# A hybrid decoder layer on one core: in 27 panels an accumulating DMA makes the low part of one weight tile in four

## Chip, core and metric

One NeuronCore of a Trainium2 chip runs the whole layer (batch 1, 256 tokens, width 1024). The metric is device time of one execution in microseconds (us): 602.37 us before the change, the median of three runs (602.12 to 602.67).

## What is computed

The reference is one layer, in float32:

```python
h  = rms_norm(x, ln1_g)
q, k, v, z, xbc, dt_raw, gate_a, gate_b = split(h @ w_in)
y_a = moba_attention(rms(q), rms(k), v) @ w_o_attn
y_b = mamba2_mixer(z, xbc, dt_raw, ...) @ w_o_ssm
x  = x + (sigmoid(gate_a) * y_a + sigmoid(gate_b) * y_b) @ w_out
h2 = rms_norm(x, ln2_g)
g, u = split(h2 @ w_gate_up)
x  = x + (silu(g) * u) @ w_down
x  = x + (p @ w_ple_proj) * sigmoid(rms_norm(x, ln3_g) @ w_ple_gate)
```

Nearly all of the arithmetic is products of 256 tokens with weight matrices of 1024 or more rows, about 100 MB of weights in all.

## The kernel before

**Products in two parts.** TensorE takes its operands as float32r, a rounded float32. To keep precision, the kernel splits each weight W into a high part Wh (W rounded) and a low part Wl = W - Wh, and each activation likewise into Ah and Al. A product A W is then three matmuls into the same PSUM bank: Ah Wh, Ah Wl and Al Wh. The names in the code and in the profile are `wh`, `wl`, `raw` (the weight as it was loaded) and `s` (all the activations, tiles of the tag `s4`).

**Panels.** The weights are cut into panels of 512 output columns and 1024 rows. A panel has eight k blocks of 128 rows. It is computed for two token tiles of 128, so it takes 8 x 2 x 3 = 48 matmuls of 128x512 into two PSUM tiles `g`. The class `Panel` (L333) does this: `add` (L345) walks over four k blocks, `step` (L365) issues the three matmuls of one block for one token tile. The loop at L903 runs over the panels of the input projection (`PANELS`, L34: xbc, q, k, v, z and the gates; an entry `yb` is a shorter panel of the mixer's output projection, done in `ssm_out`, L863). The loop at L1041 runs over the panels 2 to 10 of gate and up of the feed-forward part, here called the FFN panels. The panels of attention output, `w_out`, `w_down` and the last projection are written out elsewhere.

**Loads and splits.** A chunk of four k blocks comes as two DMAs of 512 KB (two k blocks each) into `raw`, from SyncE's queue (L275, in `load`, L269). For each tile ScalarE writes `wh` by a rounding copy (`act`, L151) and VectorE writes `wl` by a subtraction (`split_w`, L260, the subtraction at L263). There are 4 buffers for `raw`, 3 for `wh` and 6 for `wl` (L256 to L258).

**Order of the work.** Between the matmuls of the panels stand the smaller steps of the layer: transposes (L192, by a product with `ident`), the products of attention and of the scan, each waiting for ScalarE and VectorE. A `Filler` (L78) interleaves them: after each step of a panel `fill.step()` runs one piece of a waiting task, if its delay has passed on a counter of matmul time (`fill.now`). The table `LAG` (L68) holds these delays in ns. Panel matmuls keep their order among themselves (`main=True`). A scheduler then fixes the order of each engine's queue by priorities and its own clock.

**GpSimd** does little: a power of -0.5 for the norms (L381, L571) and masks for the scan (L635).

Of the kernel before, what the change touches and what calls it, by code (L numbers as in the profile page):

```python
# [10 lines left out]
F32 = mybir.dt.float32  # L11
F32R = mybir.dt.float32r
AF = mybir.ActivationFunctionType
ALU = mybir.AluOpType
AX = mybir.AxisListType

P = 128
T = 256
# [47 lines left out]


LAG = {  # L68
    "dt": 9198, "dt.t": 3823, "dt.e": 24762, "dt.low": 2074, "dt.end": 6965, "xbc": 3815, "xbc.t": 1507,
    "xbc.end": 7967, "z": 7477, "z.t": 2878, "z.end": 2196, "qk": 21856, "qk.t": 1263, "qk.end": 1856,  # L70
    "v": 3215, "cb": 0, "rows": 538, "prep": 3126, "seg": 492, "seg.next": 11553, "out": 13590,
    "out.xdt": 4839, "out.end": 90, "off": 3340, "off.end": 560, "finish": 6082, "finish.ones": 3453,
    "sc": 6834, "sc.tr": 2218, "tr": 0, "tr.val": 759, "val": 2876, "val.end": 3654, "m": 1401, "res": 4378,
    "ff": 1875, "ff.end": 1668,
}


# [31 lines left out]
def tile_layer(ctx: ExitStack, tc: tile.TileContext, head, xk, pt, vec, w_dt, w_big, w_dn2, w_pp, out):  # L109
    nc = tc.nc  # L110
# [3 lines left out]
    @contextmanager  # L114
    def prio(c):
        saved = tc.cur_priority
        tc.cur_priority = counters[c]
        yield
        counters[c] = tc.cur_priority
        tc.cur_priority = saved  # L120

    const = ctx.enter_context(tc.tile_pool(name="const", bufs=1))
    sb = ctx.enter_context(tc.tile_pool(name="sb", bufs=1))
    psg = ctx.enter_context(tc.tile_pool(name="psg", bufs=4, space=bass.MemoryType.PSUM))
    psb = ctx.enter_context(tc.tile_pool(name="psb", bufs=4, space=bass.MemoryType.PSUM))
    fill = Filler()
    uid = [0]

    def nm(s):
        uid[0] += 1  # L130
        return f"{s}_{uid[0]}"

    def s4(shape, dt=F32):
        return sb.tile([P] + shape, dt, tag="s4", bufs=26, name=nm("s4"))
# [15 lines left out]
    def act(o, i, f=AF.Copy, **kw):  # L150
        return nc.scalar.activation(o, i, f, **kw)  # L151
# [4 lines left out]
    def queue(ins, main):  # L156


        if fill.last is not None:
            follow(ins, fill.last)  # L160
        if main:
            fill.last = ins
# [6 lines left out]
    def mm(o, lhsT, rhs, start, stop, main=False):  # L169
        ins = nc.tensor.matmul(o, lhsT, rhs, start=start, stop=stop).ins  # L170
        queue(ins, main)
        passes = 4 if lhsT.dtype == F32 else 1
        fill.now += passes * max(107.0, rhs.free_size() / 2.4)
        return ins
# [58 lines left out]
    v = const.tile([P, V_N], F32, name="vecs")  # L233
# [19 lines left out]
    chunk_no = [0]  # L253

    def w_tiles():
        return (sb.tile([P, 2, 512], F32, tag="raw", bufs=4, name=nm("raw")),  # L256
                sb.tile([P, 2, 512], F32R, tag="wh", bufs=3, name=nm("wh")),
                sb.tile([P, 2, 512], F32R, tag="wl", bufs=6, name=nm("wl")))  # L258

    def split_w(tiles, js=slice(0, 2), c=WHOLE):  # L260
        raw, wh, wl = (t[:, js, c] for t in tiles)
        rounded = act(wh, raw)
        nc.vector.tensor_sub(wl, raw, wh.bitcast(F32))  # L263
        return rounded

    def parts_of(tiles):
        return [(tiles[1][:, j], tiles[2][:, j]) for j in range(2)]

    def load(src, nk):  # L269

        with prio("w"):
            parts = []
            for k in range(0, nk, 2):
                tiles = w_tiles()
                nc.sync.dma_start(tiles[0], src[:, k : k + 2])  # L275
                split_w(tiles)
                parts += parts_of(tiles)
        return parts
# [38 lines left out]
    def next_chunk():  # L317
        c = w_big[chunk_no[0]]
        chunk_no[0] += 1
        return load(c, 4)  # L320


    hh = [s4([4, T], F32R) for _ in range(2)]
    hl = [s4([4, T], F32R) for _ in range(2)]
    h_act = [(hh[k // 4][:, k % 4], hl[k // 4][:, k % 4]) for k in range(8)]

    def split_h(k):
        g = g1[:, k : k + 1]
        xk_ = xraw[k // 2][:, k % 2] if k else x0[:, 8:]
        tc.keep_in_program_order(act(h_act[k][0], xk_, scale=g))  # L330
        stt(h_act[k][1], xk_, g, h_act[k][0].bitcast(F32), op0=ALU.mult, op1=ALU.subtract)

    class Panel:  # L333

# [10 lines left out]
        def add(self, parts, acts, last):  # L345
            n = len(parts)
            if last:
                runs = [(pc, k) for pc in self.pieces for k in range(n)]
            else:
                runs = [(pc, k + j) for k in range(0, n, 2) for pc in self.pieces for j in range(2)]  # L350
            for pc, k in runs:
                self.step(pc, parts[k], acts[k], last and k == n - 1)

        def open(self, part, act_, cs):

            for w, w_acts in zip(part, (act_[:2], act_[:1])):
                for c in cs:
                    for a in w_acts:
                        for tt, _, ps in self.pieces:
                            with prio("mm"):  # L360
                                mm(ps[:, c], a[:, tt * P : tt * P + P], w[:, c], w is part[0] and a is act_[0] and c is cs[0] and id(self.pieces[tt]) not in self.begun, False, main=True)
            self.begun.update(id(pc) for pc in self.pieces)
            fill.step()
# [499 lines left out]
    def ssm_out(g):  # L863

        fill.drain(lambda: g in y_hl)
        yh, yl = y_hl[g]
        for n in range(2):
            if g == 0:
                accs[n] = s4([2, 512])
            acc = accs[n]  # L870
            pan = Panel()
            pan.add(next_chunk(), [(yh[:, k], yl[:, k]) for k in range(4)], last=True)
            with prio("ev"):
                for tt in range(2):
                    r = r_ssm[:, g, tt : tt + 1]
                    if g == 0:
                        act(acc[:, tt], pan.ps[tt], scale=r)
                    else:
                        stt(acc[:, tt], pan.ps[tt], r, acc[:, tt], op0=ALU.mult, op1=ALU.add)

    def evacuate(kind, i, pan):
        gen = evac[kind](kind, i, pan)
        t = next(gen)
        fill.spawn(gen, 0, t - fill.now)
# [3 lines left out]
    for k in range(0, 8, 2):  # L888
# [3 lines left out]
        for ks, bs in ([((k,), (0, 1)), ((k + 1,), (0, 1))] if k < 4 else [((k, k + 1), (0,)), ((k, k + 1), (1,))]):  # L892
            for b in bs:
# [6 lines left out]
                if k == 6:  # L900
                    evacuate(*PANELS[b][:2], pans[b])

    for kind, i, _ in PANELS[2:]:  # L903
        if kind == "yb":
            ssm_out(i)
            continue
        pan = Panel()
        for hf in range(2):
            pan.add(next_chunk(), h_act[4 * hf : 4 * hf + 4], last=hf == 1)
        evacuate(kind, i, pan)  # L910


# [35 lines left out]
    for n in range(2):  # L948
        pan = Panel()
# [56 lines left out]
    for n in range(2):  # L1006
        pan = Panel()
# [6 lines left out]
    ff = []  # L1014
# [23 lines left out]

    pair(res2.acts, evac_gu)
    h2 = res2.acts[0] + res2.acts[1]  # L1040
    for i in range(2, NFF):  # L1041
        pan = Panel()
        for hf in range(2):
            pan.add(next_chunk(), h2[4 * hf : 4 * hf + 4], last=hf == 1)
        evac_gu(i, pan)

    res3 = Residual(xin, V_G3, rstd3)
    for n in range(2):
        pan = Panel()
# [92 lines left out]
```

## Time and profile before

| | |
|---|---|
| Median of 3 runs (lowest, highest) | 602.37 us (602.12, 602.67) |
| Span of the profiled execution | 600.7 us, about 1.7 us under the median, for what lies around the span |
| TensorE busy, weight loads busy | 593.9 us (99%), 484.6 us (81%) |
| VectorE busy | 424.1 us (71%) |
| ScalarE busy | 338.6 us (56%) |
| GpSimd busy | 38.7 us (6%) |
| DMA | 103.88 MB, mean 173 GB/s |
| Granted TensorE clock | 1.000 |

In the profile, PE is TensorE's matmuls, PEld its weight loads, DVE VectorE, ACT ScalarE, POOL GpSimd, and SPq SyncE's queue, which issues the loads. A matmul's row lasts longer than the distance to the next one, because matmuls are pipelined; the pace is read from the starts.

### The profile page before, as it was taken

The numbers are of one execution on the slowest core, as the hardware profiler recorded it, in microseconds if no ns is written. First come the engines' busy times: TensorE is split into PE (matmuls) and PEld (weight loads), VectorE is DVE, ScalarE is ACT, GpSimd is POOL, SyncE is SP. The second block draws the span as 40 slices with busy tenths as digits, with TensorE's granted clock in tenths as the row PEclk, the third lists the DMA queues.
The fourth block names the chain that finished last, engine by engine and source line by source line (L and its number), as shares of the span: only waits on it lengthen the run. The fifth ranks groups of instructions, "written<-read, shape, count | busy, mean of one in ns | idle before, by whom it ended". The sixth has DMA issues, their size and how long they took to land.

```text
span 600.7 us, 8147 instructions
## 1 busy us (share of the span) xinstructions
PE 593.9 (99%) x2965; PEld 484.6 (81%) x2965; DVE 424.1 (71%) x668; ACT 338.6 (56%) x513; POOL 38.7 (6%) x47
## 2 busy tenths in 40 slices
PE   8999999999999999999999999999999999999997
PEld 7888888787777878887787788888888888888886
DVE  5689999978997765677875475756756666646465
ACT  6766666556775545576646444755544544445353
POOL 2000103412010011101000000000000000000000
PEclk9999999999999999999999999999999999999999
DMA  8945644533444445555544475556565555555641
GB/s 278 323 152 175 210 142 142 174 131 117 140 127 149 143 150 170 187 166 160 162 161 164 139 232 188 185 165 208 163 200 188 161 201 187 190 188 182 201 141 70
DMA packets 31192, 103.88 MB, mean 173 GB/s; under 512 B 3568, under 2 KB 4912, under 8 KB 31152
## 3 DMA queue, kind: packets, MB, share of 16 engines
q1 hardware_dynamic: 31152, 103.36, 53.3%
q8 instruction: 23, 0.38, 0.3%
q14 instruction: 17, 0.14, 0.1%
HBM read 102.23 MB, written 1.05 MB: 172 GB/s over the span
## 4 chain that ended last, share of the span: by engine, by line
PE 96%; DVE 1%; DMA 1%; ACT 0%; SPq 0%; issue 0%; ACTq 0%
PE g L170 85%; PE pb L170 6%; PE pb L192 5%; DMA raw<-in_head 1%; SPq L248 0%; DVE s L750 0%; ACT wh L151 0%; DVE s L658 0%; ACT s L151 0%; DVE wl L263 0%; DVE s L785 0%; DVE s L663 0%; DVE s L742 0%; DVE s L1063 0%; DVE s L1064 0%
## 5 line engine op out<-in xcount | busy, mean ns | idle before, releaser
L170 PE MATMUL g<-wh,s 128*128 128x512 f32 (+1 forms) x1508 | 486.7, 395 | 0.6 <-ACT wh L151 0.6
L170 PEld LDWEIGHTS g<-wh,s 128*128 128x128 f32 x1508 | 282.7, 189 | 59.6 <-issue 1.8
L263 DVE TENSOR_TENSOR wl<-raw,wh 128x1024 fp32r<-128x1024 f32 (+2 forms) x193 | 230.4, 1196 | 129.6 <-ACT wh L151 127.0
L151 ACT ACTIVATE wh<-raw 128x1024 fp32r<-128x1024 f32 (+2 forms) x193 | 199.9, 1038 | 177.7 <-PE g L170 149.8
L170 PE MATMUL g<-wl,s 128*128 128x512 f32 (+1 forms) x754 | 294.2, 392 | 0.0
L170 PEld LDWEIGHTS g<-wl,s 128*128 128x128 f32 x754 | 142.1, 189 | 27.8 <-issue 1.0
L151 ACT ACTIVATE s<-pb 128x512 f32<-128x512 f32 (+4 forms) x64 | 33.6, 544 | 30.4 <-PE pb L192 16.1
L192 PEld LDWEIGHTS pb<-ident,s 128*128 128x128 f32 x302 | 37.9, 140 | 11.4 <-issue 0.9
L192 PE MATMUL pb<-ident,s 128*128 128x128 f32 x302 | 47.1, 272 | 0.0
L151 ACT ACTIVATE s<-g,rstd 128x512 f32<-128x512 f32 (+1 forms) x50 | 28.5, 583 | 20.5 <-PE g L170 18.7
L520 DVE SCALAR_TENSOR_TENSOR s<-pb,vecs,s 128x255 f32<-128x255 f32 (+2 forms) x72 | 32.0, 475 | 1.4 <-ACT s L151 1.2
L170 PE MATMUL pb<-s,s 128*64 128x128 f32 (+6 forms) x328 | 32.6, 304 | 0.4 <-ACT s L151 0.4
L151 ACT ACTIVATE s<-pb,vecs 128x256 f32<-128x256 f32 (+2 forms) x48 | 25.9, 550 | 11.1 <-PE pb L192 5.0
L170 PEld LDWEIGHTS pb<-s,s 128*64 128x64 f32 (+2 forms) x328 | 23.1, 154 | 9.9 <-issue 4.7
L381 POOL TENSOR_TENSOR rstd<-tiny,mhalf 128x2 f32<-128x2 f32 x3 | 2.3, 762 | 315.2 <-DVE tiny L380 295.3
L151 ACT ACTIVATE s<-s 128x512 f32<-128x512 f32 (+3 forms) x24 | 19.0, 792 | 4.3 <-DVE s L978 4.0
L571 POOL TENSOR_TENSOR tiny<-tiny,mhalf 128x8 f32<-128x8 f32 x8 | 16.0, 1995 | 73.2 <-DVE tiny L569 73.2
L635 POOL TENSOR_SCALAR_AFFINE_SELECT rr<-a_h 128x512 fp32r<-128x512 f32 x16 | 13.6, 860 | 100.2 <-PE pb L170 61.7
L151 ACT ACTIVATE s<-s,tiny 128x128 f32<-128x128 f32 (+1 forms) x32 | 14.2, 444 | 6.5 <-DVE tiny L788 6.5
L1022 DVE SCALAR_TENSOR_TENSOR s<-g,rstd,s 128x256 f32<-128x256 f32 x22 | 10.6, 481 | 7.5 <-ACT s L151 7.5
L676 DVE TENSOR_TENSOR s<-s,s 128x512 f32<-128x512 f32 x16 | 11.9, 748 | 0.3 <-ACT s L151 0.3
L1023 DVE SCALAR_TENSOR_TENSOR s<-g,rstd,s 128x256 f32<-128x256 f32 x22 | 10.7, 484 | 0.7
(120 smaller groups left out, 235.2 us busy)
## 6 DMA issues: line engine op xcount, KB each, us to landing
raw<-in_w_big SPq DMA_DIRECT2D x176, 512.0 KB
raw<-in_head SPq DMA_DIRECT2D x4, 512.0 KB
s<-in_xk SPq DMA_DIRECT2D x4, 512.0 KB
raw<-in_head SPq DMA_DIRECT2D x7, 256.0 KB
raw<-in_w_pp SPq DMA_DIRECT2D x2, 512.0 KB
raw<-in_w_dn SPq DMA_DIRECT2D x2, 512.0 KB
out<-s SPq DMA_DIRECT2D x3, 256.0 KB
xraw<-in_head SPq DMA_DIRECT2D x2, 256.0 KB
```

Of the source, the lines that this page charges most:

```text
L151: return nc.scalar.activation(o, i, f, **kw)
L170: ins = nc.tensor.matmul(o, lhsT, rhs, start=start, stop=stop).ins
L192: queue(nc.tensor.transpose(o, i, ident[: i.shape[0], : i.shape[0]]).ins, False)
L263: nc.vector.tensor_sub(wl, raw, wh.bitcast(F32))
L381: nc.gpsimd.tensor_tensor(dst, t, mhalf[:, : ss.shape[-1]], op=ALU.pow)
L520: stt(cc[:, sft:], pu[:, j, : T - sft], cw[3 - sft], cc[:, sft:], op0=ALU.mult, op1=ALU.add)
L571: nc.gpsimd.tensor_tensor(f, ms, mhalf, op=ALU.pow)
L635: nc.gpsimd.affine_select(r, bcast(a_h[:, c, h0 : h0 + 4].bitcast(F32), P), pattern=[[0, 4], [1, P]], compare_op=ALU.is_ge, fill=0.0, base ...
L676: nc.vector.tensor_tensor(m, m, cbm[:, g, c].unsqueeze(1).to_broadcast([P, 4, P]), op=ALU.mult)
L1022: stt(t[:, tt], pan.ps[tt][:, :T], r, t[:, tt], op0=ALU.mult, op1=ALU.mult)
L1023: stt(t[:, tt], pan.ps[tt][:, T:], r, t[:, tt], op0=ALU.mult, op1=ALU.mult)
```

## The change

**In the 18 panels of the loop over `PANELS` and the 9 FFN panels,** `add_all` takes the place of two calls of `add`. The first of the panel's four weight tiles (k blocks 0 and 1) has no `wh` and `wl`. ScalarE writes -Wh into a tile `both` (same instruction, scale -1). GpSimd has made -Ah and -Al of the activation's first two k blocks once, in `negated`. The panel begins with eight matmuls that take these: (-Ah)(-Wh) and (-Al)(-Wh), for two k blocks and two token tiles. Then `turn()` issues a DMA on GpSimd's queue that adds `raw` into `both`, within SBUF: `both` becomes W - Wh = Wl. The 36 matmuls of the other three weight tiles follow as before. Four matmuls Ah Wl out of `both` close the panel. The number of matmuls stays 48, and VectorE's subtraction for this tile goes. `both` has 2 buffers, `wl` 5 instead of 6. The delays in `LAG` are all new numbers; two lines of the table are enough here.

```diff
 LAG = {
-    "dt": 9198, "dt.t": 3823, "dt.e": 24762, "dt.low": 2074, "dt.end": 6965, "xbc": 3815, "xbc.t": 1507,
+    "dt": 8608, "dt.t": 6654, "dt.e": 22935, "dt.low": 2265, "dt.end": 2300, "xbc": 2926, "xbc.t": 1484,
...
-                sb.tile([P, 2, 512], F32R, tag="wl", bufs=6, name=nm("wl")))
+                sb.tile([P, 2, 512], F32R, tag="wl", bufs=5, name=nm("wl")))
...
+    def next_two():
+
+        c = w_big[chunk_no[0] : chunk_no[0] + 2]
+        chunk_no[0] += 2
+        with prio("w"):
+            raw = sb.tile([P, 2, 512], F32, tag="raw", bufs=4, name=nm("raw"))
+            both = sb.tile([P, 2, 512], F32R, tag="both", bufs=2, name=nm("both"))
+            nc.sync.dma_start(raw, c[0, :, 0:2])
+            act(both, raw, scale=-1.0)
+        parts = load(c[0, :, 2:4], 2) + load(c[1], 4)
+
+        def turn():
+            with prio("w"):
+                nc.gpsimd.dma_start(both, raw, accum_op=ALU.add)
+
+        return both, turn, parts
...
+    def negated(acts):
+
+        n = s4([2, 2, T], F32R)
+        with prio("bg"):
+            for j in range(2):
+                for m in range(2):
+                    nc.gpsimd.tensor_scalar(n[:, j, m], acts[j][m].bitcast(F32), -1.0, None, op0=ALU.mult)
+        return [(n[:, j, 0], n[:, j, 1]) for j in range(2)]
...
+        def add_all(self, acts, neg):
+
+            both, turn, parts = next_two()
+            for tt in range(2):
+                ts = slice(tt * P, tt * P + P)
+                for j in range(2):
+                    for m in range(2):
+                        with prio("mm"):
+                            mm(self.ps[tt], neg[j][m][:, ts], both[:, j], j == 0 and m == 0, False, main=True)
+                    fill.step()
+            self.begun.update(id(pc) for pc in self.pieces)
+            turn()
+            self.add(parts, acts[2:], last=False)
+            for tt in range(2):
+                ts = slice(tt * P, tt * P + P)
+                for j in range(2):
+                    with prio("mm"):
+                        mm(self.ps[tt], acts[j][0][:, ts], both[:, j], False, j == 1, main=True)
+                fill.step()
...
-        for hf in range(2):
-            pan.add(next_chunk(), h_act[4 * hf : 4 * hf + 4], last=hf == 1)
+        pan.add_all(h_act, h_neg)
...
-        for hf in range(2):
-            pan.add(next_chunk(), h2[4 * hf : 4 * hf + 4], last=hf == 1)
+        pan.add_all(h2, h2_neg)
```

How the queues stand, first **TensorE in an FFN panel.** Before, around the second half of a panel (PSUM tiles `g_848`, `g_849`); `pb` with `ident` are the transposes of the panel before it:

```order
L170 MATMUL g_849_4130<-wh_851_4132,s4_759_3664 128x512
L192 MATMUL pb_856_4152<-ident_83,s2_847_4122 128x128 x2
L170 MATMUL g_848_4129<-wh_854_4138,s4_758_3663 128x512
...
L170 MATMUL g_848_4129<-wh_859_4176,s4_774_3735 128x512
L192 MATMUL pb_856_4152<-ident_83,s2_847_4122 128x128 x2
L170 MATMUL g_848_4129<-wh_862_4182,s4_773_3734 128x512
...
L170 MATMUL g_849_4130<-wh_862_4182,s4_774_3735 128x512
L170 MATMUL g_865_4218<-wh_868_4221,s4_758_3663 128x512
L170 MATMUL g_865_4218<-wl_869_4222,s4_758_3663 128x512
```

TensorE in an FFN panel of the change (`g_862`, `g_863`; `s4_797` holds the negated activations):

```order
L170 MATMUL g_862_4295<-both_865_4298,s4_797_3938 128x512 x4
L170 MATMUL g_863_4296<-both_865_4298,s4_797_3938 128x512 x4
L170 MATMUL g_862_4295<-wh_867_4302,s4_741_3650 128x512
L170 MATMUL g_862_4295<-wl_868_4303,s4_741_3650 128x512
...
L192 MATMUL pb_875_4321<-ident_83,s2_861_4288 128x128 x4
...
L170 MATMUL g_863_4296<-wh_873_4314,s4_757_3716 128x512
L170 MATMUL g_862_4295<-both_865_4298,s4_741_3650 128x512 x2
L170 MATMUL g_863_4296<-both_865_4298,s4_741_3650 128x512 x2
L170 MATMUL g_878_4383<-both_881_4386,s4_797_3938 128x512 x4
```

Between the eighth matmul and the first closing one stand 36 matmuls of the panel and, in one run, the four transposes that stood in two pairs. In the panels of the input projection there is more between them, but for two panels (`both_468`, `both_483`), where only the 36 stand there.

**GpSimd's queue at the FFN panels.** Before, the powers of the second and third norm follow each other directly:

```order
L381 TENSOR_TENSOR r_ssm<-tiny_2792,mhalf 128x2
L381 TENSOR_TENSOR r_ssm<-tiny_2801,mhalf 128x2
L381 TENSOR_TENSOR rstd_3511<-tiny_3703,mhalf 128x2
L381 TENSOR_TENSOR rstd_3512<-tiny_5195,mhalf 128x2
L1138 UNCONDITIONAL_BRANCH
```

GpSimd's queue at the same place of the change:

```order
L427 TENSOR_TENSOR rstd_3498<-tiny_3699,mhalf 128x2
L356 TENSOR_SCALAR s_797_3938<-s_741_3650 128x256
L356 TENSOR_SCALAR s_797_3938<-s_742_3651 128x256
L356 TENSOR_SCALAR s_797_3938<-s_741_3650 128x256
L356 TENSOR_SCALAR s_797_3938<-s_742_3651 128x256
L336 DMA both_3946<-raw_3945 128x1024
L336 DMA both_4034<-raw_4033 128x1024
L336 DMA both_4122<-raw_4121 128x1024
L336 DMA both_4210<-raw_4209 128x1024
```

The four negations and nine turns are added, and among the FFN panels nothing else stands in this queue. In the input projection the masks and powers of the scan stand between the turns.

**SyncE's queue at the FFN panels of the change,** with what each load waits for (DMAHW: an earlier load's semaphore; DVE: VectorE; DMASW: a DMA that GpSimd issued):

```order
L330 DMA raw_864_4297<-in_w_big 128x1024 [waits DMAHW1_49,DVE_49]
L275 DMA raw_866_4301<-in_w_big 128x1024 [waits DMAHW2_49,DVE_49]
L275 DMA raw_869_4307<-in_w_big 128x1024 [waits DMAHW3_49,DVE_49]
L275 DMA raw_872_4313<-in_w_big 128x1024 [waits DMAHW0_49,DMASW5_49]
L330 DMA raw_880_4385<-in_w_big 128x1024 [waits DMAHW5_49,DVE_49]
```

The load of a panel's first tile is now at L330. The load of its fourth tile takes the buffer of the first tile of the panel before, and waits for that tile's turn; before, all four waited for VectorE.

More of the change, by code (lines that the diff above doesn't have):

```diff
@@ L68 @@
 LAG = {
-    "dt": 9198, "dt.t": 3823, "dt.e": 24762, "dt.low": 2074, "dt.end": 6965, "xbc": 3815, "xbc.t": 1507,
[L70 to L74, printed above, removed]
+    "dt": 8608, "dt.t": 6654, "dt.e": 22935, "dt.low": 2265, "dt.end": 2300, "xbc": 2926, "xbc.t": 1484,
+    "xbc.end": 7789, "z": 12292, "z.t": 2124, "z.end": 2000, "qk": 13028, "qk.t": 0, "qk.end": 1529, "v": 0,
+    "cb": 206, "rows": 500, "prep": 3126, "seg": 1695, "seg.next": 4000, "out": 7134, "out.xdt": 1513,
+    "out.end": 1126, "off": 1998, "off.end": 2677, "finish": 6573, "finish.ones": 3782, "sc": 8833,
+    "sc.tr": 4000, "tr": 1321, "tr.val": 0, "val": 4477, "val.end": 8000, "m": 0, "res": 2734, "ff": 243,
+    "ff.end": 2771,
 }
@@ L901, in tile_layer @@
                     evacuate(*PANELS[b][:2], pans[b])
+    h_neg = negated(h_act)
     for kind, i, _ in PANELS[2:]:
@@ L1040, in tile_layer @@
     h2 = res2.acts[0] + res2.acts[1]
+    h2_neg = negated(h2)
     for i in range(2, NFF):
         pan = Panel()
-        for hf in range(2):
-            pan.add(next_chunk(), h2[4 * hf : 4 * hf + 4], last=hf == 1)
+        pan.add_all(h2, h2_neg)
         evac_gu(i, pan)
```

## The prediction

> **What bounds the kernel now.** I read the page's busy times first, then the stretches of 25 us, then the waits of TensorE and its timeline. The page:
>
> ```profile
> span 600.7 us, 8147 instructions
> PE 593.9 (99%) x2965; PEld 484.6 (81%) x2965; DVE 424.1 (71%) x668; ACT 338.6 (56%) x513; POOL 38.7 (6%) x47
> ```
>
> TensorE is busy all the time, the others are not. The stretches show where that is least so (columns: start and end, length, then busy time of PE, PEld, DVE, ACT and POOL, granted clock, DMA share, GB/s):
>
> ```profile
> 100.00:125.00 25.00, 24.63 (x132) 19.29 (x131) 23.09 (x38) 13.58 (x18) 10.19 (x7) 1.00 0.49 163
> 150.00:175.00 25.00, 24.66 (x153) 19.28 (x152) 24.12 (x57) 18.79 (x40) 2.98 (x4) 1.00 0.41 126
> 425.00:450.00 25.00, 25.00 (x116) 20.54 (x115) 15.72 (x19) 11.92 (x15) 0.00 (x0) 1.00 0.58 189
> ```
>
> The first two are the only full stretches between 25 and 575 us in which PE is short of 25.00, by 0.37 and 0.34 us, and there VectorE is nearly full (23.09 and 24.12). In the FFN panels, third row, PE lacks nothing and VectorE has 9 us to spare. "Busy" could hide a slow pace, so I look at starts. Three rows of an FFN panel:
>
> ```profile
> 431.71 0.39 PE L170 MATMUL g<-wl,s 128*128 128x512 f32 x1
> 431.94 0.62 PE L170 MATMUL g<-wh,s 128*128 128x512 f32 x2
> 432.39 0.39 PE L170 MATMUL g<-wl,s 128*128 128x512 f32 x1
> ```
>
> From 431.71 to 432.39 are three matmuls: 0.227 us each, whichever operand it is. The count of matmuls and this pace make the time. What PE waits for elsewhere stands in two places:
>
> ```profile
> 107.58 0.39 PE L170 MATMUL g<-wh,s 128*128 128x512 f32 x1
> 108.33 0.93 PE L170 MATMUL pb<-s,s 128*64 128x128 f32 x12 [0.37 <-ACT s L151]
> 169.94 0.61 PE L170 MATMUL g<-wh,s 128*128 128x512 f32 x2
> 170.89 0.61 PE L170 MATMUL pb<-ones,s 128*128 128x1 f32 x4 [0.34 <-DVE s L744]
> ```
>
> By starts the first wait costs 0.75 - 0.227 = 0.52 us, the second (the pair's second matmul starts at 170.17) 0.72 - 0.227 = 0.49 us. So in the middle of the kernel TensorE loses 1.0 us, and no more can be won by helping another engine, unless the order of the matmuls itself packs better.
>
> **The change part by part.** Matmuls: 324 take `both` in place of `wh` or `wl`, in the same shape, each with a weight load of its own as before; 48 per panel stay 48. At 0.227 us for either operand that is 0. In the FFN panels two pairs of transposes become one run of four. Rows of both kinds in the old kernel:
>
> ```profile
> 434.66 0.39 PE L170 MATMUL g<-wh,s 128*128 128x512 f32 x1
> 434.89 0.38 PE L192 MATMUL pb<-ident,s 128*128 128x128 f32 x2
> 435.03 0.48 PE L170 MATMUL g<-wh,s 128*128 128x512 f32 x1
> 435.34 0.39 PE L170 MATMUL g<-wl,s 128*128 128x512 f32 x1
> 30.20 0.39 PE L170 MATMUL g<-wh,s 128*128 128x512 f32 x1
> 30.43 0.60 PE L192 MATMUL pb<-ident,s 128*128 128x128 f32 x4
> 30.79 0.48 PE L170 MATMUL g<-wh,s 128*128 128x512 f32 x1
> 31.10 0.40 PE L170 MATMUL g<-wl,s 128*128 128x512 f32 x1
> ```
>
> A pair takes 0.68 - 2 x 0.227 = 0.23 us, four take 0.90 - 0.45 = 0.45 us: again 0.
>
> VectorE and ScalarE, by the groups of instructions:
>
> ```profile
> L263 DVE TENSOR_TENSOR wl<-raw,wh 128x1024 fp32r<-128x1024 f32 x184 | 224.7, 1223 | 126.4 <-ACT wh L151 123.9
> L151 ACT ACTIVATE wh<-raw 128x1024 fp32r<-128x1024 f32 x184 | 194.7, 1060 | 174.5 <-PE g L170 149.8 <-issue 13.0 <-DVE wl L263 3.3
> L226 POOL TENSOR_SCALAR le_q<-s 128x128 f32<-128x128 f32 x1 | 0.5, 540 | 0.0
> 24.40 0.89 POOL L381 TENSOR_TENSOR rstd<-tiny,mhalf 128x2 f32<-128x2 f32 x1 [19.96 <-DVE eps L402]
> ```
>
> VectorE loses 27 x 1.22 = 33 us of work, off the path but for the waits above. The wait at 108 us lies among changed panels, and what it waits for comes through a full VectorE: I take its 0.5 us as won. The other lies among mixer panels, which don't change. ScalarE's copy with scale -1 replaces a copy of the same form: 0. The eight negations on GpSimd take about 2 x 0.54 = 1.1 us each for 256 columns (an estimate from the L226 row). The first four stand behind the power that ended at 25.29, so they end near 29.7; the first panel that needs them starts near 30.2, from the run of 16 small products that the old row shows:
>
> ```profile
> 27.86 2.04 PE L170 MATMUL pb<-s,s 128*64 128x256 f32 x16
> ```
>
> (27.86, plus 1.87 to the next start, plus four transposes at 0.45). That is hidden, by only half a microsecond; if it isn't, it costs that once.
>
> **The turn** is the new wait: the closing matmuls stand behind it in TensorE's queue, so all of TensorE waits if it is late. Its room in an FFN panel follows from the old panel's length:
>
> ```profile
> 429.65 0.47 ACT L151 ACTIVATE s<-g,rstd 128x256 f32<-128x256 f32 x1 [0.79 <-PE g L170]
> 441.04 0.47 ACT L151 ACTIVATE s<-g,rstd 128x256 f32<-128x256 f32 x1 [0.79 <-PE g L170]
> ```
>
> A panel is 11.39 us. Less twelve matmuls (eight ahead, four behind: 2.72) and the 0.16 us by which the eighth outlasts its successor's start (0.39 - 0.227), 8.5 us remain. The two panels with 36 matmuls alone between have 36 x 0.227 - 0.16 = 8.0 us; the others have 8.3 to 10.5, by what the order puts between.
>
> No accumulating DMA and none from GpSimd is in this trace. Nearest are SyncE's loads:
>
> ```profile
> q1 hardware_dynamic: 31152, 103.36, 53.3%
> 0.80 0.39 SPq L248 DMA_DIRECT2D x<-in_head  x1
> 2.89 0.51 ACT L151 ACTIVATE s<-x 128x256 fp32r<-128x256 f32 x1 [0.61 <-DMA x<-in_head]
> ```
>
> 53.3% of 16 engines over 600.7 us for 103.36 MB makes 1.62 us of all sixteen for 512 KB (0.524 MB). The 132 KB load, alone at its start, took 2.09 us to its user, of which 0.42 is moving at that rate: 1.7 us are fixed. A plain 512 KB DMA would thus take 1.62 + 1.7 = 3.3 us, the lower end. An accumulation reads two tiles and writes one; if it passes three times and gets only what the loads leave (58% busy in the row of 425 us), it takes 3 x 1.62 / 0.42 + 1.7 = 13.3 us, the upper end. I take two passes, sharing engines half and half while loads run: 3.24 / (1 - 0.29) + 1.7 = 6.3 us, since the loads show an engine's time going by bytes read. That fits into 8.0 with 1.7 us to spare, so the turn costs 0.
>
> [...]
>
> Behind the turn: the fourth tile's load of the next panel waits for it in SyncE's queue, and later loads wait behind that. The turn ends near 1.8 + 6.3 = 8.1 us into a panel; load 3.3, copy 1.06 and subtraction 1.22 end by 13.8. Its first use is 32 matmuls into the next panel, at 11.4 + 7.3 = 18.7. So 5 us to spare. On GpSimd's queue the scan's powers and masks can delay a turn in the input projection:
>
> ```profile
> L571 POOL TENSOR_TENSOR tiny<-tiny,mhalf 128x8 f32<-128x8 f32 x8 | 16.0, 1995 | 73.2 <-DVE tiny L569 73.2
> 115.27 2.63 POOL L571 TENSOR_TENSOR tiny<-tiny,mhalf 128x8 f32<-128x8 f32 x1 [3.67 <-DVE tiny L569]
> ```
>
> One power ahead makes 6.3 + 2.6 = 8.9 us at worst; the panels among them have 9 us or more of room. Hidden, narrowly.
>
> **Step delays.** They move small products between panel matmuls. The waits of PE above are what such placing costs now, 1.0 us. From a gain of all of it to a loss of 3 us (a pair of such waits in each of three stages), I take 0, as the order keeps both kinds of runs.
>
> Sum: 600.7 + 1.7 (to the median 602.4) - 0.5 = 601.9 us. A difference under 0.2%, or 1.2 us, is about what a measurement can't tell from none.
>
> **The rivals.**
>
> *Late turn (slower).* The closing matmuls wait for the DMA. It decides from 8.0 us on for two panels and 8.5 for the FFN panels. For it: three passes, or a long way through GpSimd; against it: the loads' row, and room of 1.7 us. At 9.5 us: nine FFN panels x 1.0, two x 1.5, the other sixteen about 0.3 each: 9 + 3 + 5 = 17, so 619 us. Each further us adds up to 27.
>
> *Better packing (faster).* Both waits go, and the new order also saves part of what weight loads lose around small products:
>
> ```profile
> PEld pb L170 <- issue: 4.7, 15, 0.4
> PEld g L170 <- issue: 2.8, 15, 0.2
> ```
>
> A quarter of these 7.5 us and the 1.0 make 2.9 at most, 2.0 with half of the packing: 600.4 us. Against it: loads overlap matmuls, so idle there is not all lost.
>
> [...]
>
> *Shorter delays make new waits (slower).* Several delays fall to 0, so a product may stand before its operand is ready: six waits of 0.5, 605 us.
>
> That the edit doesn't do what it says is excluded by the order: 27 turns stand in GpSimd's queue.
>
> **How the numbers follow.** Hidden turn, 601.9 (its own range 600.7 to 603.4): 0.50, of which 0.40 within 1.2 us of the old time, 0.07 faster, 0.03 slower. Late turn 0.18, better packing 0.23, VectorE 0.04, new waits 0.05. Faster 0.07 + 0.23 = 0.30; same 0.40; slower 0.03 + 0.18 + 0.04 + 0.05 = 0.30. The range goes from 600.0, below which I leave about a third of the better packing (0.07), to 612, above which lies two thirds of the late turn (0.12).
>
> **What would show it.** In the changed profile: starts 0.227 us apart also at `both`; VectorE's subtractions down to 157, its busy time near 391 us; between GpSimd's issue of a turn and the first closing matmul no idle time of PE, and no wait of PE for a DMA. I am wrong if PE lists waits for `both` by DMA (late turn), if the wait at 108 us stays, or if PE waits for ScalarE or VectorE in new places.

## The result, and the profile after

| | before | after |
|---|---|---|
| Median (lowest, highest; runs) | 602.31 us (602.12, 602.67; 4) | 608.69 us (605.79, 609.32; 4) |
| After / before, 95% interval | | 1.0095 (1.0073 to 1.0117) |
| Profiled execution, its span | 602.37, 600.7 us | 609.32, 607.6 us |

The change makes the kernel 1.0% slower, and its runs no longer agree: 3.5 us lie between them, where the runs before lay within 0.6. A second set of seven runs (h4 below) gave 606.36 us, 1.0067 (1.0042 to 1.0093). One of the 24 runs of before in that set, at 1532 us, is left out of all comparisons as slow.

The page after, its first two lines:

```profile
span 607.6 us, 8177 instructions
PE 596.9 (98%) x2965; PEld 484.7 (80%) x2965; DVE 391.8 (64%) x641; ACT 332.1 (55%) x513; POOL 72.6 (12%) x82
```

VectorE lost 32 us of work, as it should, and PE's count of matmuls is what it was. The stretches of 25 us show where the time is (columns as in the prediction):

```profile
100.00:125.00 25.00, 22.93 (x115) 17.59 (x112) 21.16 (x38) 13.18 (x17) 9.99 (x6) 0.93 0.60 168
225.00:250.00 25.00, 24.48 (x112) 19.93 (x111) 8.19 (x8) 9.74 (x11) 1.73 (x3) 1.00 0.72 197
400.00:425.00 25.00, 23.80 (x110) 19.31 (x109) 13.86 (x18) 13.96 (x17) 0.93 (x1) 1.00 0.64 192
425.00:450.00 25.00, 25.00 (x116) 20.71 (x115) 11.47 (x16) 10.81 (x15) 1.71 (x2) 1.00 0.76 212
```

The last row is the steady state of the FFN panels: PE lacks nothing, though the DMA share rose from 0.58 to 0.76. In the others PE is short by 2.1, 0.5 and 1.2 us, and in the first the clock is under 1. TensorE's waits name them (in all, times, longest, in us):

```profile
PE pb L170 <- ACT s L151: 2.1, 1, 2.1
PE pb L192 <- DVE s L1069: 1.2, 1, 1.2
PE pb L205 <- DVE ones L209: 1.1, 1, 1.1
PE g L170 <- DVE s L618: 0.7, 1, 0.7
PE g L170 <- DMA both<-raw: 0.5, 1, 0.5
PE g L170 <- ACT wh L151: 0.5, 1, 0.5
```

Each stands once (the third is the program's start, there before as well). So the loss is a handful of single waits, not a price per panel. By the starts of all 2965 matmuls, the intervals more than 0.15 us longer than the pace of their shape (its median) have 13.7 us above it, before 7.4: 6.3 of the 6.9 us by which the span grew. Into the 13.7 goes the half clock that follows the largest wait (3.41 us at clock 0.50). This is that one, at 110 us (start, length, engine, instruction, then in brackets idle time and its releaser):

```profile
110.01 0.73 PE L170 MATMUL g<-both,s 128*128 128x512 f32 x2
111.21 1.06 ACT L151 ACTIVATE both<-raw 128x1024 fp32r<-128x1024 f32 x1 [1.22 <-DMA raw<-in_w_big]
112.17 1.06 ACT L151 ACTIVATE s<-pb 128x512 f32<-128x512 f32 x2
112.81 1.60 PE L170 MATMUL pb<-s,s 128*128 128x512 f32 x2 [2.07 <-ACT s L151]
```

ScalarE stands 1.22 us at the copy into `both`, whose load is late. Behind it in ScalarE's queue is the step that TensorE's next matmul needs. ScalarE's waits for loads from `in_w_big`, before and then after:

```profile
ACT wh L151 <- DMA raw<-in_w_big: 1.0, 1, 1.0
```

```profile
ACT wh L151 <- DMA raw<-in_w_big: 71.2, 29, 5.9
ACT both L151 <- DMA raw<-in_w_big: 18.5, 13, 2.3
```

and SyncE's queue, which issues these loads, after:

```profile
SPq L275 <- DVE wl L263: 262.3, 107, 7.1
SPq L275 <- DMA both<-raw: 140.5, 27, 10.5
```

Behind each of the 27 turns the next load stands for 5 us in the mean. Before, ScalarE waited once for such a load; now it waits 42 times.

### The profile page after: what moved, and what is told of

The parts are those of the page before. It is cut to its first block, busy times and chain, and to the rows that moved or that the text cites. A ratio compares the mean times of both kernels' runs of the same rounds, so it can differ in the third digit from the quotient of the medians.

```text
span 607.6 us, 8177 instructions
## 1 busy us (share of the span) xinstructions
PE 596.9 (98%) x2965; PEld 484.7 (80%) x2965; DVE 391.8 (64%) x641; ACT 332.1 (55%) x513; POOL 72.6 (12%) x82
## 3 DMA queue, kind: packets, MB, share of 16 engines
q0 software_dynamic: 3888, 14.16, 12.6%
## 4 chain that ended last, share of the span: by engine, by line
PE 80%; DMA 8%; DVE 6%; issue 2%; ACT 2%; POOL 1%; SPq 0%; ACTq 0%; POOLq 0%; DVEq 0%
PE g L170 70%; PE pb L170 5%; DMA raw<-in_w_big 5%; PE pb L192 5%; DMA both<-raw 2%; DVE s L566 2%; DVE wl L263 1%; ACT wh L151 1%; POOL tiny L617 1%; DMA raw<-in_head 1%; ACT s L151 1%; ACT both L151 1%; DVE s L572 1%; DVE s L722 0%; SPq L248 0%
## 5 line engine op out<-in xcount | busy, mean ns | idle before, releaser
L170 PE MATMUL g<-wh,s 128*128 128x512 f32 (+1 forms) x1292 | 416.1, 394 | 0.5 <-ACT wh L151 0.5
L263 DVE TENSOR_TENSOR wl<-raw,wh 128x1024 fp32r<-128x1024 f32 (+2 forms) x166 | 197.3, 1192 | 161.7 <-ACT wh L151 161.1
L170 PEld LDWEIGHTS g<-wh,s 128*128 128x128 f32 x1292 | 241.0, 188 | 51.4 <-issue 2.0
L151 ACT ACTIVATE wh<-raw 128x1024 fp32r<-128x1024 f32 (+2 forms) x166 | 171.2, 1033 | 191.6 <-PE g L170 95.2
L170 PE MATMUL g<-wl,s 128*128 128x512 f32 (+1 forms) x646 | 251.5, 391 | 0.0
L170 PEld LDWEIGHTS g<-wl,s 128*128 128x128 f32 x646 | 121.3, 188 | 24.5 <-issue 0.7
L170 PE MATMUL g<-both,s 128*128 128x512 f32 x324 | 85.0, 399 | 1.2 <-DVE s L618 0.7
L170 PEld LDWEIGHTS g<-both,s 128*128 128x128 f32 x324 | 59.7, 189 | 15.1 <-issue 2.0
L336 POOL DMA_DIRECT2D both<-raw x27 | 23.9, 886 | 250.2 <-PE g L170 95.7
L151 ACT ACTIVATE both<-raw 128x1024 fp32r<-128x1024 f32 x27 | 28.6, 1058 | 18.7 <-DMA raw<-in_w_big 18.5
L170 PEld LDWEIGHTS pb<-s,s 128*64 128x64 f32 (+2 forms) x328 | 23.4, 154 | 13.7 <-issue 5.7
```

The costliest lines, as they stand in the source:

```text
L336: nc.gpsimd.dma_start(both, raw, accum_op=ALU.add)
```

## The experiments

I held three theories in turn. **A:** the buffer of `raw` that the turn holds makes loads late, ScalarE's queue stands, TensorE waits. **B:** the new delays leave small products too little slack. **C:** the copy into `both` stands too early in ScalarE's queue, since it waits for no buffer that TensorE frees. (In the expectations of e1 to e4 "rival C" is another one: the turn's traffic slows the loads.) Each kernel's time is a median, with the ratio to before on the same chip and its 95% interval. One table shows where a trace stands against before, by the start of the first matmul of the same panel (us later than before). A number can fall again further down, since the orders place different small products ahead of a panel:

| start in before | after | h4, after again | f1 | e3 | h3 | h1 |
|---|---|---|---|---|---|---|
| 106.4 | 2.3 | 3.1 | 2.5 | 2.8 | 3.1 | -0.6 |
| 122.0 | 5.7 | 5.0 | 1.8 | 2.2 | 2.5 | -0.6 |
| 333.0 | 5.7 | 5.8 | 0.5 | 1.4 | 1.4 | -0.7 |
| 409.1, first changed FFN panel | 5.6 | 5.7 | 0.6 | 1.5 | 1.2 | -0.5 |
| 420.8, second | 6.9 | 7.0 | 2.6 | 8.3 | 1.2 | 1.0 |
| 511.9 | 6.8 | 6.8 | 2.9 | 9.5 | 1.2 | 0.8 |

### The two halves of the change (e1, e2)

e1 is the kernel before with the new table `LAG`; e2 is the changed kernel with the old one.

```diff
 LAG = {
-    "dt": 9198, "dt.t": 3823, "dt.e": 24762, "dt.low": 2074, "dt.end": 6965, "xbc": 3815, "xbc.t": 1507,
...
+    "dt": 8608, "dt.t": 6654, "dt.e": 22935, "dt.low": 2265, "dt.end": 2300, "xbc": 2926, "xbc.t": 1484,
...
```

> The kernel before with only the new step delays. Theory A (a raw buffer is held by the turn, so later loads come late, ScalarE's queue stands still at them, and TensorE then waits for what stands behind): 601 to 603 us, ScalarE's waits for the loads stay near 1 us in all. Rival B (the new delays put products ahead of their operands): 606 to 609 us, with PE waits for ScalarE or VectorE of some 5 us. Rival C (the 14 MB of added DMA traffic slow the loads): 601 to 603 us.

> The changed panels with the old step delays. Theory A: 605 to 610 us, ScalarE waiting over 50 us in all for weight loads. Rival B: 601 to 603 us. Rival C: as A, 605 to 610 us.

e1: 616.17 us, 1.0231 (1.0216 to 1.0246). e2: 624.95, 1.0375 (1.0337 to 1.0413). Each half alone costs more than both together. The new panels are worth +22.6 us with the old table and -7.5 with the new one, and the new table +13.8 or -16.3. So a table of delays has no price of its own. In e1 there is no turn, and ScalarE waits 1.6 us in all for loads from `in_w_big`, yet TensorE has this:

```profile
PE pb L192 <- DVE s L572: 5.4, 2, 3.6
PE pb L192 <- ACT s L151: 2.1, 1, 2.1
```

### Without the held buffer, without the DMA (e3, e4)

```diff
-            raw = sb.tile([P, 2, 512], F32, tag="raw", bufs=4, name=nm("raw"))
+            raw = sb.tile([P, 2, 512], F32, tag="raw", bufs=5, name=nm("raw"))
```

e3 does this in both places that name the tag. e4 makes the turn an addition on VectorE:

```diff
-                nc.gpsimd.dma_start(both, raw, accum_op=ALU.add)
+                nc.vector.tensor_tensor(both, raw, both.bitcast(F32), op=ALU.add)
```

> The changed kernel with a fifth buffer for raw; its TensorE order stays nearly the same. Theory A: 602 to 604 us, ScalarE's waits for weight loads fall from 90 us to under 30. Rival B: 608 us, since the order is the same. Rival C: 606 to 609 us, since the bytes stay.

> The changed kernel with the turn as one VectorE addition (both = both + raw) instead of the DMA: raw is free some 1.3 us after the eighth matmul instead of 7 to 8, and the added bytes are gone. Theory A: 602 to 604 us. Rival B: 607 to 609 us. Rival C: 602 to 604 us.

e3: 612.53 us, 1.0174 (1.0157 to 1.0191), slower than the change. But the table shows two things: up to the FFN panels only 1.5 us are lost, where the change lost 5.6, and 7 us come in one place, with a half clock of 6.8 us behind it:

```profile
PE pb L192 <- DVE s L1069: 4.2, 1, 4.2
```

e4: 607.29, 1.0083 (1.0068 to 1.0099). Without any DMA 5 us are lost all the same, in waits behind ScalarE and VectorE between 107 and 128 us and in the same transposes (1.3 us). So a kernel without a turn's DMA loses nearly as much, which speaks against the turn's traffic, and against A as the only cause. It rules out neither: the scheduler sees the other buffers, and each of these kernels has an order of its own (TensorE's differs from the changed kernel's from 59 us on in e4, from 177 us on in e3).

### The FFN stage's wait, and loads (f1 to f4)

f1 is the changed kernel with one old delay; f2 has five buffers besides:

```diff
-    "sc.tr": 4000, "tr": 1321, "tr.val": 0, "val": 4477, "val.end": 8000, "m": 0, "res": 2734, "ff": 243,
+    "sc.tr": 4000, "tr": 1321, "tr.val": 0, "val": 4477, "val.end": 8000, "m": 0, "res": 2734, "ff": 1875,
```

f3 gives the tile of the turn two buffers of its own (`tag="rawb", bufs=2`, the four of `raw` kept). f4 writes the turn behind the second weight tile:

```diff
-            turn()
-            self.add(parts, acts[2:], last=False)
+            self.add(parts[:2], acts[2:4], last=False)
+            turn()
+            self.add(parts[2:], acts[4:], last=False)
```

> The changed kernel with one delay of the old table: "ff" 1875 in place of 243, so the four transposes of an FFN panel come 1.6 us later in TensorE's order; nothing else, and up to the FFN panels the order is the same. Theory B (short delays leave small products no slack): the wait of 1.36 us of the transposes for VectorE at the first changed FFN panel goes, 608.7 becomes about 607.3, and all that was lost before the FFN panels (5.6 us) stays. Theory A (only the buffer held by the turn counts): ScalarE stands 2 us for a late load there whatever the delay, the wait stays or moves to the next product, 608 to 609.

> The changed kernel with five buffers for raw and "ff" 1875. Five buffers alone took 612.5, with one wait of 4.2 us and 6.8 us at half clock at the first changed FFN panel, and 1.3 us lost up to there. Both theories together: the transposes stand 1.6 us later, the wait shrinks to 2.6 us or goes; if it goes, the half clock goes too: 610.4 - 4.5 - 3.0 = 603 of span, 604.5 of time. If late loads alone make that wait (theory A), it only shrinks by 1.6 and stays above 2 us: 609 to 610.

> The changed kernel, but the tile that the turn reads has two buffers of its own, and the four of raw serve the other three tiles, so that no load stands behind a turn in SyncE's queue unless it is itself two panels ahead. Theory A: what was lost before the FFN panels (5.6 us) shrinks to about 1, and ScalarE's waits for loads (90 us in all) fall under 30: 603 to 605 unless a wait remains at the first FFN panel. Theory B: the waits stay where the delays put them, 607 to 609.

> The changed kernel with the turn issued twelve matmuls (2.7 us) later, behind the second weight tile's matmuls. If a turn takes 6.5 us from issue to landing, as its median in the profile is, an FFN panel has 8.5 - 2.7 = 5.8 us for it: TensorE waits some 0.7 us for the DMA in each of nine FFN panels, 1.2 in each of the two panels without small products, less in the others, 9 to 15 us in all: 618 to 624, with waits of closing matmuls for both by DMA in the list. If a turn really needs only about 5.5 us, no such waits, 608 to 610, and the late turn had 3 us to spare.

f1: 606.31 us (605.41 to 608.71), 1.0073 (1.0049 to 1.0097). The wait did not go, it is 1.9 us. But the edit did not move the pair of transposes that waits to a later place, as expected: it stands behind the panel's 19th matmul of 128x512, in the changed kernel behind the 21st. So f1 is no test of B. Another thing in this trace matters more: up to the last 5 us ahead of the FFN panels its order is that of the changed kernel, instruction by instruction on every engine, and it lost 0.6 us there, not 5.6. ScalarE waited as long for its loads (73.2 and 11.6 us), but not where TensorE was next. **The wait at 110 us is thus not set by the order alone: it depends on when single loads land in that execution.** f2: 607.98, 1.0092 (1.0067 to 1.0117), a wait of 2.3 us left at the transposes and two late turns (1.1). f3: 611.64 (607.09 to 615.45), 1.0152 (1.0099 to 1.0206), 2.7 us at the transposes; ScalarE's waits for loads from `in_w_big` fell to 12.3, and the time did not follow. f4: 609.42, 1.0110 (1.0078 to 1.0142), and it tells nothing of a late turn: GpSimd waits only for the eight matmuls, so it issued where it did before (3.42 us behind the start of the run of twelve `both` matmuls in both kernels: 441.55 against 438.13, and 439.21 against 435.79). The order of every engine is the changed kernel's, so f4 is one more execution of it; its column of the table would be 4.5, 4.4, 3.4, 3.4, 4.6, 6.4.

### Moving ScalarE's copy back (g1 to g4)

```diff
+            self.add(parts[:2], acts[2:4], last=False)
+            set_mark()
+            self.add(parts[2:], acts[4:], last=False)
...
-            act(both, raw, scale=-1.0)
+            if mark:
+                with tc.issue_after(mark[-1]):
+                    act(both, raw, scale=-1.0)
```

`set_mark` keeps the ScalarE instruction that was written out last, and the next panel's copy is queued behind it. g1 does this in the changed kernel, g2 with five buffers, g3 with f3's buffers, g4 with e4's turn.

> The changed kernel, but ScalarE's copy into both is kept in its queue behind the ScalarE step that was written out last when the panel before had done its second weight tile. Buffers, DMA, delays as changed. Theory C (the copy into both waits for no buffer that TensorE frees, so it was queued nearly a panel ahead, stands there for its load, and what is queued behind it comes late): ScalarE's waits for raw by both fall from 18.5 us to under 5, TensorE's waits behind ScalarE and VectorE at 110 and 420 us go, 602.5 to 604.5, and the runs lie within 1.5 us of each other. Theory B (short delays): no change of these waits, 607 to 609, spread of 3 us as now.

> As g1_pin, with five buffers for raw. Theory C with the buffer that the turn holds as a second cause: no wait of ScalarE for loads over 2 us is left, 601.5 to 604, and the wait of 4.2 us at the first changed FFN panel that five buffers alone showed is gone. Theory B: that wait stays, 609 to 613.

> As g1_pin, with two buffers of their own for the tile that the turn reads (six in all). Theory C: as g2_pin_raw5, 601.5 to 604, but a wait of about 1 us for GpSimd's negations at 31 us, as with own buffers alone. Theory B: the wait of 2.9 us at the first changed FFN panel stays, 607 to 612.

> As g1_pin, with the turn as an addition on VectorE in place of the DMA (27 additions of 1.2 us). Theory C: with the copy in its place there is nothing left of the 5 us that this kernel lost without a DMA; the additions cost what the subtractions did: 602 to 604. If it is equal to g1_pin, the DMA itself costs nothing here. Theory B: 606 to 608 as without the pin.

All four missed: 624.65 us, 1.0367 (1.0332 to 1.0401); 613.12, 1.0195 (1.0164 to 1.0226); 619.54, 1.0280 (1.0263 to 1.0297); 612.70, 1.0175 (1.0160 to 1.0190). The first half of C held: in g1 ScalarE waits 2.7 us for loads at this copy, where it waited 18.5. The second didn't: the copy now comes too late, and TensorE waits for it directly:

```profile
PE g L170 <- ACT both L151: 7.3, 4, 4.2
PE pb L192 <- DVE s L1080: 3.0, 2, 2.7
PE pb L192 <- ACT both L151: 3.0, 1, 3.0
```

Nor did the wait of the first FFN transposes go (second row; the line number is shifted). There the pin did what it should, no copy into `both` stands ahead of the evacuation any more, and the wait is 2.7 us in all four. So at this place C can't be the whole cause; what is, the next section shows.

### The change divided by stage (h1 to h4)

h1 has the old loop in the input projection and all old delays, and the new panels in the FFN loop alone; h2 has the old FFN loop in the changed kernel; h3 is h2 with five buffers; h4 is the changed kernel once more. Up to the FFN panels TensorE's order in h1 is that of before, in h2 that of after.

```diff
-        pan.add_all(h2, h2_neg)
+        for hf in range(2):
+            pan.add(next_chunk(), h2[4 * hf : 4 * hf + 4], last=hf == 1)
```

is h2's edit, and h1 has the same one at the other loop, with `h_act`.

> The kernel before with the new panels in the nine FFN panels alone, and with all of its old delays (wl with 5 buffers); up to the FFN panels each engine has the order of before. My prediction's terms (matmuls 0, turn hidden, delays unchanged): 602 to 603. If the new panel brings a wait of its own at the first changed FFN panel, as it did in all kernels so far, whatever the delay, buffers or turn (1.3 to 4.5 us, and 3.4 us at half clock where it is above 2 us): 603.5 to 609, and the other eight FFN panels free.

> The changed kernel with the old panels in the FFN loop; up to there each engine has the order of the changed kernel. What the input projection costs is then alone: if the waits at 110, 241 and 256 us of the changed kernel's profile come in every run, 606.5 to 607.5 with under 1 us between the runs. If they are a matter of when loads land in one run, as the kernel with one new delay, the same up to there, shows by losing only 0.6 us, then 603 to 607, with 2 us or more between the runs.

> As h2_proj_only, with five buffers for raw. Five buffers alone lost 1.4 us up to the FFN panels: 603 to 604.5, with under 1 us between the runs, if the buffer held by the turn is what makes the input projection's time vary. If it isn't, as h2_proj_only, 605 to 607 with 2 us or more between the runs.

> The changed kernel itself, once more, with another profile. If its waits are a matter of when loads land, the waits at 110, 241 and 256 us are others or missing this time, the wait of 1.4 us at 420 us is there again, and the runs lie between 605 and 610. If they are set by the order, the same four waits stand at the same places with the same lengths.

h1: 604.25 us, 1.0034 (1.0023 to 1.0045), so +2.2. The table's last column says where, for the profiled execution (603.64 us, the fastest of eight): 1.5 us in the first changed panel, and nothing in the eight behind it. What the slower ones lose besides, no trace shows. This is the cleanest place to read the cause. Before, from the end of the panel ahead:

```profile
407.98 1.06 ACT L151 ACTIVATE wh<-raw 128x1024 fp32r<-128x1024 f32 x1 [0.91 <-PE g L170]
409.35 1.06 ACT L151 ACTIVATE wh<-raw 128x1024 fp32r<-128x1024 f32 x1 [0.30 <-PE g L170]
410.32 0.45 ACT L151 ACTIVATE s<-g,rstd 128x256 f32<-128x256 f32 x1
412.58 0.48 DVE L1023 SCALAR_TENSOR_TENSOR s<-g,rstd,s 128x256 f32<-128x256 f32 x1
416.45 0.38 PE L192 MATMUL pb<-ident,s 128*128 128x128 f32 x2
```

and h1, whose clock stands 0.7 us ahead of that:

```profile
405.35 0.33 SPq L330 DMA_DIRECT2D raw<-in_w_big  x1
407.32 1.06 ACT L151 ACTIVATE wh<-raw 128x1024 fp32r<-128x1024 f32 x1 [0.91 <-PE g L170]
408.63 2.08 PE L170 MATMUL g<-both,s 128*128 128x512 f32 x8
410.19 1.06 ACT L151 ACTIVATE both<-raw 128x1024 fp32r<-128x1024 f32 x1 [1.81 <-DMA raw<-in_w_big]
411.16 1.04 ACT L151 ACTIVATE wh<-raw 128x1024 fp32r<-128x1024 f32 x1
412.11 0.45 ACT L151 ACTIVATE s<-g,rstd 128x256 f32<-128x256 f32 x1
414.37 0.47 DVE L1069 SCALAR_TENSOR_TENSOR s<-g,rstd,s 128x256 f32<-128x256 f32 x1
414.90 0.44 PE L192 MATMUL pb<-ident,s 128*128 128x128 f32 x2 [1.44 <-DVE s L1069]
```

Before, each copy waits for TensorE to free a buffer of `wh`, its load long landed. In h1 the copy into `both`, for the panel after this one, waits for no TensorE buffer. It stands ahead of the evacuation `s<-g` of the last panel and waits 1.81 us for a load issued 4.84 us earlier. From the copy `wh` that both have, the evacuation comes 4.79 us later instead of 2.34, VectorE's step 7.05 instead of 4.60, and the transposes wait 1.44 us.

That is one half. The other is the place of these transposes in TensorE's order: before, they stand behind the 30th matmul of 128x512 of the panel and start 7.3 us after its first one, when VectorE's step has long ended. In h1 they stand behind the 19th and are due at 4.8 us. With the old place the late step would have been in time, and with the old step the early place. The two shifts in other kernels (us after the start of the first changed FFN panel; the wait is that of this pair of transposes):

| | behind matmul | evacuation starts | VectorE's step ends | transposes due | wait |
|---|---|---|---|---|---|
| before | 30 | 1.17 | 3.91 | 7.31 | none |
| h1 | 19 | 3.48 | 6.21 | 4.83 | 1.44 |
| after | 21 | 3.65 | 6.39 | 5.25 | 1.20 |
| i2 (below) | 26 | 3.17 | 6.10 | 6.26 | none |
| e3 | 3 | 2.38 | 5.31 | 1.16 | 4.21 |
| f3, g1 to g4 | 3 | 1.03 | 3.76 | 1.16 | 2.66 |

In f3 and g1 to g4 no late load stands ahead of the evacuation, and the step ends as early as before. The wait is there all the same, by the place alone; in f3 (its panel starts at 411.30):

```profile
412.33 0.46 ACT L151 ACTIVATE s<-g,rstd 128x256 f32<-128x256 f32 x1
414.59 0.47 DVE L1069 SCALAR_TENSOR_TENSOR s<-g,rstd,s 128x256 f32<-128x256 f32 x1
415.12 0.44 PE L192 MATMUL pb<-ident,s 128*128 128x128 f32 x2 [2.66 <-DVE s L1069]
```

At the same place, the late load of e3 adds 1.55 us.

h2: 604.34 (603.17 to 605.85), 1.0034 (1.0020 to 1.0047), so +2.2 as well, with 2.7 us between the runs. h3: 603.71 (603.19 to 603.94), 1.0023 (1.0014 to 1.0032). The median moved little, but its ten runs lie within 0.75 us: **with a fifth buffer the variation is gone** (the runs of before in that set lie within 1.7), and TensorE's list is short:

```profile
PE pb L205 <- DVE ones L209: 1.1, 1, 1.1
PE g L170 <- DVE wl L263: 0.8, 2, 0.7
```

Near 110 us h3 has h2's order on TensorE, and ScalarE's copy into `both` waits for no load. But its queues are ordered otherwise elsewhere, ScalarE's from 20 us on and TensorE's from 177 us on, so buffer and order are not told apart.

h4: 606.36 (604.45 to 610.45). The same places as in the first profile, with other lengths: 1.5 us at 111 us in place of 2.1, without a half clock there (1.00 from 108 to 120 us), but the time up to 333 us is the same. Five traces have one order up to there. ScalarE's wait for the load at this copy, and TensorE's wait behind it:

| | after | h4 | f4 | h2 | f1 |
|---|---|---|---|---|---|
| ScalarE at `both` for the load, us | 1.22 | 0.62 | 0.99 | 1.07 | none |
| TensorE behind ScalarE, us | 2.07 | 1.47 | 0.30 | 0.36 | none |

So the order sets where TensorE can be caught, and the landing of loads sets whether; how long it waits also depends on what came late ahead of this copy. The parts come near the whole, 2.2 + 2.2 = 4.4 against 4.3 in h4 and 6.4 in the first four runs, but that is partly chance: h1 has the old delays, and so another order in the FFN panels than the changed kernel.

### The transposes later, with and without a fifth buffer (i1, i2)

i1 is h1 with `"ff": 4000`, i2 the changed kernel with five buffers and `"ff": 5000`.

> As h1_ffn_only (604.25), with "ff" 4000 in place of 1875: the four transposes come 2.1 us later in TensorE's order, behind the end of the VectorE step that they waited 1.4 us for. If that one wait is all that the FFN panels cost, and the new panel, its turn and its buffers are free otherwise: it goes, 602.2 to 603.0. If the wait only moves to another product: 604 to 605.

> The changed kernel with five buffers for raw and "ff" 5000, 4.8 us later than changed. Five buffers took the projection's loss down to 1.2 to 1.4 us, and the wait of the FFN stage's first transposes (4.2 us with five buffers) should go with its half clock: 602.09 + 1.6 = 603 to 604.5, under 1.5 us between the runs. If late turns remain in FFN panels, as five buffers showed twice (0.6 us each): 604 to 606.

i1: 604.36 us, 1.0041 (1.0029 to 1.0053), no change: the first pair of the transposes moved from behind the 11th matmul to behind the 20th, but the pair that waits moved by one, from the 19th to the 20th, and waits 1.4 us for VectorE as it did. i2: 606.98, 1.0078 (1.0062 to 1.0094). Here the late load is still ahead of the evacuation, but the transposes stand behind the 26th matmul, and their wait is gone:

```profile
410.46 1.06 ACT L151 ACTIVATE both<-raw 128x1024 fp32r<-128x1024 f32 x1 [2.71 <-DMA raw<-in_w_big]
416.19 0.60 PE L192 MATMUL pb<-ident,s 128*128 128x128 f32 x4
```

TensorE now waits for turns instead:

```profile
PE g L170 <- DMA both<-raw: 1.9, 3, 0.8
```

The turns' times from issue to landing between 410 and 520 us, of the changed kernel and then of i2:

```profile
DMA to landing us min/median/max: 4.8/6.0/7.9
```

```profile
DMA to landing us min/median/max: 5.8/8.1/8.9
```

With a free buffer more of the loads run beside a turn: by the DMA packets, 2.3 loads' worth of bytes in the mean during a turn of i2, 1.5 during one of the changed kernel. The turns take 2 us longer, the longest of them past the 8.5 us that a panel leaves. I read this as the loads slowing the turn, which the held buffer had kept apart. No version ran faster than the kernel before; the best with the new panels in any place is h3, 1.6 us above it.

## Why the prediction was wrong

I forecast 601.9 us, no change that can be measured; it was 608.7 and 606.4. By its steps:

- **Matmuls, 0: right.** Eight FFN panels take 511.9 - 420.8 = 91.1 us before and 518.7 - 427.7 = 91.0 after.
- **The turn, 6.3 us and hidden: nearly right.** Its median is 6.5 us. In the first trace TensorE waits for it once, 0.5 us, in one of the two panels without small products (8.1 us there); in the other traces with this order up to 400 us the waits for it are 0.2 to 1.3 us in all. The rival of the late turn fell in its size, but i2 shows that its bound was near: at 8.1 us in the FFN panels it begins to cost (1.9 us in three waits). Its load on the engines was well estimated too:

```profile
q0 software_dynamic: 3888, 14.16, 12.6%
q1 hardware_dynamic: 31152, 103.36, 52.1%
both<-raw POOLq DMA_DIRECT2D x27, 512.0 KB, 6.5
```

12.6% of 607.6 us over 27 turns is 2.84 us of all sixteen engines each, 1.8 times the 1.61 of a load; I had taken two passes, 3.24. My reason, that an engine's time goes by bytes read, no run shows, since a load's row does not part reading from writing; what the runs show is the 1.8. Nor does any show the fixed 1.7 us by itself: that was my estimate from one small load, issued at 0.80 us and in use at 2.89, with other loads issued from 1.25 us on. Measured are whole turns, the shortest of the changed kernel 4.8 us.
- **VectorE, 33 us less and 0.5 us won: the first right (32.3), the second wrong.** Near 110 us TensorE waits longer than before, 2.1 us for ScalarE; of the five traces with this order only f1's has no wait there.
- **"ScalarE's copy with scale -1 replaces a copy of the same form: 0": this step failed.** The form is the same, the place in the queue is not. Before, a copy into `wh` waits for TensorE, and its load has long landed; the copy into `both` has a spare buffer and waits for its load, with the evacuation queued behind it. In h1 this makes the evacuation 2.45 us later; in the changed kernel, at 110 us, TensorE waits 2.1 us behind such a copy.
- **"So 5 us to spare" behind the turn: wrong as well.** I followed the fourth tile to its first use by TensorE, and not to ScalarE's queue, where a late load holds up everything behind it. ScalarE's waits for loads from `in_w_big` went from 1 to 90 us. Most hit nothing; in the projection a few hit TensorE, and which ones differs between executions. In h3, with one buffer more and an order partly its own, that variation is gone.
- **Step delays, "I take 0, as the order keeps both kinds of runs": this step failed too.** I compared how long the transposes take, 0.45 us either way, and not how far they stand behind the step that they need. The order moved the waiting pair from behind the 30th matmul of the panel to behind the 21st, 19th or 3rd: this alone made 2.66 us of wait with nothing late (f3, g1 to g4), and in h1 and the changed kernel it took the slack of 3.4 us that would have hidden the late evacuation. Bounded by -1 and +3, the new table is worth +13.8 us alone and -16.3 with the new panels: it can't be costed without them.
- **Negations, hidden by half a microsecond: right** in the changed kernel. In f3, with two more buffers for loads, TensorE waits 1.2 us for GpSimd's negations.

The nearest rival was new waits, 605 us, which I gave 0.05. Its sign and its kind were right: TensorE waits for ScalarE and VectorE in new places, and in the first FFN panel a product stands before its operand is ready. That single delays of 0 do this was not shown: the old `ff` delay in f1 moved the waiting pair to an earlier place. For the chance of 0.04 called VectorE no run has a figure; the changed kernel shows the turn's median, 6.5 us against 6.3 forecast.

Open remain 1.3 us of span in h3 for which the list of TensorE's waits has nothing, and why the order has the waiting transposes behind the 21st matmul in the changed kernel and behind the 3rd in e3, with the same delays. In the projection the chain is read from five traces of one order; no run took the late loads away and kept the order.

## What to carry to other kernels

When an in-order engine gets a copy with a new destination, ask what that copy waits for now: one that waited for its consumer left its load time to land, and one with a spare buffer moves ahead in the queue until it waits for the load, with everything behind it (ScalarE's waits for loads from `in_w_big`: 1.0 us before, 89.7 after). Follow a longer-held buffer to the first engine that stands behind the delayed load, not to the last user. When a change reorders a queue, compare for each small product how far it stands behind its operand, before and after: a wait can come from a later operand (2.07 us at 110 us in the changed kernel, none in f1 with the same order there), an earlier place (2.66 us in f3), or only from both together (1.44 us in h1). And when the runs of a kernel begin to spread (0.6 us before, 3.5 after), lost slack is a thing to look for.

## What the hardware showed that I had not expected

A wait of TensorE cost more here than its length. After the 2.24 us gap at 110 us, the clock fell (a stretch of the changed kernel, columns as above, the granted clock third from the end):

```profile
113.30:116.70 3.40, 3.40 (x12) 2.61 (x11) 3.15 (x6) 1.67 (x3) 0.22 (x1) 0.50 0.43 146
```

3.41 us at half clock, some 1.7 us of work; after the 4.5 us gap in e3, 6.8 us. There was none after a gap of 1.64 us (h4), and none after 2.24 us in e1 (at 94 us) or 2.91 us in f3 (clock 1.00 from 412 to 421 us), so length alone doesn't decide, and the 2 us in the expectation of h1 are no bound. What decides, no trace here shows.
